# A two-layer decoder trunk on one core: attention steps respaced, rotary chain split, one weight tile requested earlier, output written in four pieces

## The chip, the core and the metric

The kernel runs on one core of a Trainium2 chip. A core has a matrix engine (TensorE, PE in the profile, with its weight loads as PEld), a vector engine (VectorE, DVE), an activation engine (ScalarE, ACT), a general engine (GpSimd, POOL) and a queue engine that issues transfers (SyncE, SP). The engines run side by side, each takes its own instructions in order, and they wait for each other by semaphores. The metric is the device time of one execution in microseconds; lower is better.

## What is computed

Two layers run over 256 tokens of width 2048, in float32. Of the reference this is the part that the change touches:

```python
h = rms_norm(x, attn_norm[l])
z = h @ w_in[l]
za, zq, zk, zv, zc = jnp.split(z, SPLIT_IDX, axis=-1)
ya = gmlp_mixer(za, ...)            # gelu, layer norm, 128 x 128 token mixing
yb = diff_attention(zq, zk, zv, lam, cos, sin)   # 4 heads, q and k turned by cos and sin
yc = short_conv_mixer(bg, cg, hc, conv_w[l])
x = x + (mix * mix_norm[l]) @ w_out[l]           # mix = group norms of ya, yb, yc
h = rms_norm(x, ffn_norm[l])
x = x + (jax.nn.silu(h @ w_gate[l]) * (h @ w_up[l])) @ w_down[l]
...
return rms_norm(x, final_norm)
```

`cos` and `sin` are taken of position times inverse frequency. `rms_norm` divides each token by the root of the mean of its squares, so each token has one scale `r`.

## The kernel before

**Weights.** All weights (some 420 MB) come from HBM once, as tiles of 512 by 512 numbers (1 MB each, `wf`), at most four of them in SBUF. Each tile is cut into two halves. For each half ACT rounds the weights (`wh`, line 169), DVE takes the difference to the exact ones (`wl`, line 170), and PE makes 12 matmuls of 512 columns (lines 220 to 222): for two token blocks of 128 and two rows of blocks, activations high part times `wh`, times `wl`, and activations low part times `wh`. One half with its 12 matmuls is called a step here, and the steps are numbered from 0. `wh` and `wl` have five buffers, so ACT can start the half of step n + 5 when PE has finished step n.

**Order of the work.** Eight steps make one chunk of 512 output columns of the first projection. Its chunks come in the order v, v (steps 0 to 15, interleaved), q and k of head pair 0 (16 to 31), q and k of head pair 1 (32 to 47), the gMLP's second half (48 to 55), the convolution's three parts (56 to 79) and the gMLP's first half (80 to 87). Then come the output projection and the feed-forward part. All the smaller work stands in one list (`pending`, filled by `later(fn, key, wait, gap)`): after each step `step()` takes at most one entry off its front, no sooner than `wait` steps after it was put there and `gap` steps after the last one ran; `need(key)` runs the list until an entry is done.

**What the scheduler does.** The kernel text is not the order of the program. A scheduler that knows the dependencies places the instructions on the engines, and it may pull an instruction ahead of another one on the same engine that stands earlier in the text.

**Attention of a head pair** (`attention`, line 633 on). Four entries `scores` (line 647: product `sp` of keys `bok` and queries `boq`; then mask, maximum, exponent and normalisation, `se` and `st`, on DVE and ACT), then five entries `turn`: transposes `ap` on PE, a copy, products `op` with the values (line 679), group norms with two small POOL instructions (lines 339 and 340). `bok` and `boq` are made by ACT and DVE copies of 32 partitions (lines 456 and 458). The gMLP's `vg` (gelu, line 727), its statistics (`bst`, `mv`), POOL's power `rs` and the normalised `vn` (line 737, then POOL's lines 740 and 741) fall beside the scores of pair 1.

**Start.** `load_weights` and the loads of the transposed input quarters (`xt`, line 308) are issued by SP in the order of the text. POOL works out the rotary angles in some fifty small instructions (`rotary_tables`, lines 346 to 385), and then the token scales `r` (`token_scales`, by `rstd`, lines 339 and 340), for which `v` on ACT (line 707) and `rq` on DVE (line 608) wait.

**End.** After the last products, for each of the two token blocks: residual add and squares (lines 884 and 886), sum, POOL's scale and power, a scaling of two halves of 1024 columns by DVE and ACT (lines 895 and 897), and two transfers of 512 KB (line 898).

Of the kernel before, what the change touches and what calls it, by code (L numbers as in the profile page):

```python
# [11 lines left out]
F32 = mybir.dt.float32  # L12
# [3 lines left out]
ALU = mybir.AluOpType  # L16
AX = mybir.AxisListType

P = 128
D = 2048  # L20
S = 256
NT = S // P
L = 2
CW = 512
# [3 lines left out]
RMS_EPS = 1e-6  # L28
# [25 lines left out]
def trunk_kernel(ctx: ExitStack, tc, x, positions, w_in, gmlp_ln_g, gmlp_ln_b,  # L54
# [8 lines left out]
    nc = tc.nc  # L63
# [75 lines left out]
    def load_weights(n):  # L139
        while state["load"] < min(n, len(wsrc)):  # L140
            i = state["load"]
            wf = wfp.tile([P, 4, CW], F32, tag="wf", name=f"wf{i}")
            w = 2 if i < 4 else 4
            for k in range(0, 4, w):
                nc.sync.dma_start(out=wf[:, k:k + w], in_=wsrc[i][:, k:k + w])
            wfull[i] = wf
            state["load"] += 1
# [41 lines left out]
    def later(fn, key=None, wait=0, gap=0):  # L189

        pending.append((fn, key, clock["now"] + wait, gap))
# [112 lines left out]
    for c in range(NX):  # L304
        xt = blk([P, 4, S], f"xt{c}")
        th, tl = blk([P, 4, S], f"tha0_{c}", F32R), blk([P, 4, S], f"tla0_{c}", F32R)
        for k in range(0, 4, 2):
            nc.sync.dma_start(out=xt[:, k:k + 2], in_=x_t[c, :, k:k + 2])
            if c == 0:
                if k == 0:  # L310
                    nc.sync.dma_start(out=gT, in_=gains)
                load_weight_part(0, 1 + k, 2 + k)
                if k == 0:
                    load_weight_part(0, 2, 3)
            g = [gT[:, 4 * c + kk:4 * c + kk + 1] for kk in range(4)]
            for kk in range(k, k + 2):
                if c == 0:
                    nc.vector.tensor_scalar(th[:, kk], xt[:, kk], g[kk], None, op0=ALU.mult)
                else:
                    nc.scalar.activation(th[:, kk], xt[:, kk], AF.Copy, scale=g[kk])  # L320
            if c == 0:
                split_weights(1 + k // 2)
            for kk in range(k, k + 2):
                nc.vector.scalar_tensor_tensor(tl[:, kk], xt[:, kk], g[kk], th[:, kk].bitcast(F32),
                                               op0=ALU.mult, op1=ALU.subtract)
            if c == 1 and k == 0:
                tabs = load_tables()
        stat[("a0", c)] = (th, tl)
        done.add(("a0", c))
        load_weights(min(c + 1, 3))  # L330

    mask = cpool.tile([P, 2 * P], F32, name="mask")
    nc.gpsimd.memset(mask, 0.0)
# [3 lines left out]
    def rstd(dst, src, scale, eps, n):  # L337

        nc.gpsimd.tensor_scalar(dst, src, scale, eps, op0=ALU.mult, op1=ALU.add)
        nc.gpsimd.tensor_tensor(dst, dst, neghalf[:, :n], op=ALU.pow)  # L340

    def rotary_tables(pos_i, frq):
        V = nc.gpsimd

        def axpy(dst, a, c, b):
            V.tensor_scalar(prod, a, c, None, op0=ALU.mult)
            V.tensor_tensor(dst, prod, b, op=ALU.add)

        pos = spool.tile([P, NT], F32, name="pos", bufs=1)
        V.tensor_copy(pos, pos_i)  # L350
        tmp = blk([P, 8, NT * 64], "rtmp")
        ang, far, n, acc, rem, prod = (tmp[:, j, :] for j in range(6))
        for t in range(NT):
            V.tensor_scalar(ang[:, t * 64:(t + 1) * 64], frq, pos[:, t:t + 1], None, op0=ALU.mult)
        big = 2.0 ** 18
        V.tensor_scalar(far, ang, 1.0 / big, MAGIC, op0=ALU.mult, op1=ALU.add)
        V.tensor_scalar(far, far, MAGIC, None, op0=ALU.subtract)
        axpy(ang, far, -big, ang)
        cs = _parts(TWO_PI, 8, 3)
        cs.append(float(np.float32(TWO_PI - sum(cs))))  # L360
        fm = _far_mod()
        fs = _parts(abs(fm), 8, 3)
        fs.append(float(np.float32(abs(fm) - sum(fs))))
        if fm < 0:
            fs = [-v for v in fs]

        def turns(src, scale):
            V.tensor_scalar(n, src, scale / TWO_PI, MAGIC, op0=ALU.mult, op1=ALU.add)
            V.tensor_scalar(n, n, MAGIC, None, op0=ALU.subtract)

        turns(far, fm)
        V.tensor_scalar(rem, far, fs[0], None, op0=ALU.mult)
        axpy(rem, n, -cs[0], rem)
        for j in range(1, 4):
            axpy(rem, far, fs[j], rem)
            axpy(rem, n, -cs[j], rem)
        turns(ang, 1.0)
        for j in range(4):
            axpy(ang, n, -cs[j], ang)
        V.tensor_tensor(ang, ang, rem, op=ALU.add)  # L380
        turns(ang, 1.0)
        for j in range(4):
            axpy(ang, n, -cs[j], ang)
        lim = 3.1415925
        V.tensor_scalar(ang, ang, lim, -lim, op0=ALU.min, op1=ALU.max)

        def waves():
            with tc.issue_after(state["dve"].ins):
                nc.vector.scalar_tensor_tensor(acc, ang, -1.0, ang, op0=ALU.mult, op1=ALU.max)
                nc.vector.tensor_scalar(acc, acc, -1.0, math.pi / 2, op0=ALU.mult, op1=ALU.add)  # L390
            with tc.issue_after(state["act"].ins):
                nc.scalar.activation(sinT.rearrange("p t d -> p (t d)"), ang, AF.Sin)
                nc.scalar.activation(cosT.rearrange("p t d -> p (t d)"), acc, AF.Sin)

        return waves


    neglam = cpool.tile([P, L], F32, name="neglam")
# [19 lines left out]
    def layer_loads(l):  # L418
        lc = [blk([P, 2, CW], f"lc{l}_{j}") for j in range(3)]
        wT = lc[0][:, 0].rearrange("p (g c) -> p g c", g=4)  # L420
        lng, lnb = lc[1][:, 0], lc[1][:, 1]
        cw = [lc[0][:, 1], lc[2][:, 0], lc[2][:, 1]]

        def gmlp():
            nc.sync.dma_start(out=wT, in_=ws_t[:, l])
            nc.sync.dma_start(out=lng, in_=gmlp_ln_g[l].rearrange("g c -> (g c)").partition_broadcast(P))
            nc.sync.dma_start(out=lnb, in_=gmlp_ln_b[l].rearrange("g c -> (g c)").partition_broadcast(P))
            nc.gpsimd.affine_select(out=wT, in_=wT, compare_op=ALU.is_ge, fill=0.0, base=0,
                                    pattern=[[0, 4], [1, P]], channel_multiplier=-1)

        later(gmlp, gap=2)
        def conv():
            for k in range(3):
                nc.sync.dma_start(out=cw[k], in_=conv_w[l, k].partition_broadcast(P))

        later(conv, gap=2)
        return lng, lnb, cw, wT
# [148 lines left out]
        later(lambda c=c: load_x(c), wait=5)  # L586
    for c in range(NX):
        later(lambda c=c: sum_squares(c, ssq))
    waves = rotary_tables(*tabs)

    for l in range(L):

# [18 lines left out]
                    nc.vector.tensor_scalar(rt[:, t, j, 1], sinT[:, t], sc, None, op0=ALU.mult)  # L611

        later(token_scales, ("r", l))
        lng, lnb, cw, wT = layer_loads(l)
        if l == 0:
            later(lambda: lambdas(load_lambda()))
        later(rotary_scales, ("rt", l), wait=17 if l == 0 else 0)

        def rotate(acc, j, name):

# [14 lines left out]
        def attention(pair, qT, kT, v):  # L635
# [52 lines left out]
                parts.append((scores, values, mixed))  # L688
            order = [(hh, i) for hh in range(2) for i in range(NT)]
            for hh, i in order:  # L690
                later(lambda i=i, f=parts[hh][0]: f(i), wait=2)
            for n in range(5):
                def turn(n=n):
                    if n:
                        parts[order[n - 1][0]][2](order[n - 1][1])
                    if n < 4:
                        parts[order[n][0]][1](order[n][1])
                later(turn)
            block_transposed(oy, M, key, 64 + 16 * l + 4 * (1 + pair), wait=2)

        vn = mx = xc_ = yconv = None
# [177 lines left out]
    flush()  # L879
    ov = out[0].rearrange("(t p) d -> p t d", p=P)  # L880
    c = NX - 1
    for t in range(NT):
        xc = xs[:, t, c * CW:(c + 1) * CW]
        nc.vector.tensor_tensor(xc, xc, acc[t], op=ALU.add)
        junk = spool.tile([P, CW], F32, tag="junk", name="junk", bufs=1)
        nc.scalar.activation(junk, xc, AF.Square, accum_out=ssq[:, t, c:c + 1])
        r = spool.tile([P, 2], F32, tag="rl", name="rl")
        nc.vector.tensor_reduce(r[:, 0:1], ssq[:, t], axis=AX.X, op=ALU.add)
        rstd(r[:, 1:2], r[:, 0:1], 1.0 / D, RMS_EPS, 1)
        rr = r[:, 1:2]  # L890
        nc.vector.tensor_tensor(xf[t][1][:, 1], xc, fin[1][:, 1], op=ALU.mult)
        for h in range(2):
            o = xf[t][h]
            if h == 0:
                nc.vector.tensor_scalar(o, o, rr, None, op0=ALU.mult)
            else:
                nc.scalar.activation(o, o, AF.Copy, scale=rr)
            nc.sync.dma_start(out=ov[:, t, 2 * h * CW:2 * (h + 1) * CW].rearrange("p (c n) -> p c n", c=2), in_=o)


_INS = ["x", "positions", "w_in", "gmlp_ln_g", "gmlp_ln_b", "lambda_q1", "lambda_k1", "lambda_q2",
# [39 lines left out]
```

## Time and profile before

| | |
|---|---|
| median of 3 runs | 2122.61 us (2120.73 to 2123.92) |
| profiled execution | 2121.89 us, of which its span 2119.8 us |
| PE busy | 2098.0 us, 99% of the span |
| DVE, ACT, POOL busy | 1559.2, 1137.6, 201.0 us |
| read from HBM | 423.19 MB |

The span runs from the first instruction to the last event of the profiled execution; the execution's own time is 2.1 us longer. PE is busy nearly throughout, so what can be gained without taking work off PE lies where PE waits: at the start, at the end and at the few places where its next operand is late. The view of waits lists these, the timeline places them, and the windows give the clock that PE was granted (1.00 is the upper level of 2.4 GHz).

### The profile page before, as it was taken

How to read it: one execution, taken by the hardware profiler on the slowest of the kernel's cores; microseconds unless marked ns; L12 is line 12 of the kernel's file. 1: busy time of each engine (PE TensorE's matmuls, PEld its weight loads, DVE VectorE, ACT ScalarE, POOL GpSimd, SP SyncE). 2: the span in 40 equal slices, each digit the busy share in tenths (PEclk: the TensorE clock that was granted, in tenths of full speed). 3: DMA queues.
4: the chain of work that ended last, by engine and by line, in shares of the span. 5: the costliest groups of instructions: out<-in, count | busy, mean ns of one | idle time of the engine just before them, and what ended most of it. 6: DMA issues, size and time to landing. Idle time of an engine off the chain costs nothing.

```text
span 2119.8 us, 25036 instructions
## 1 busy us (share of the span) xinstructions
PE 2098.0 (99%) x9264; PEld 1735.2 (82%) x9264; DVE 1559.2 (74%) x1926; ACT 1137.6 (54%) x1479; POOL 201.0 (9%) x199
## 2 busy tenths in 40 slices
PE   8999999999999999999999999999999999999998
PEld 7887888888888888888888878888888888888886
DVE  5787778877567775678767878788775678756874
ACT  6556468555444543454755664675554454534453
POOL 6123410000000000000001234000000000000002
PEclk9999999999999999999999999999999999999999
DMA  8654555676556656566565445556655566655663
GB/s 317 240 177 161 179 211 176 219 250 218 199 180 245 220 203 221 205 222 204 204 235 190 160 158 197 201 186 247 219 200 220 207 220 215 227 204 208 212 231 123
DMA packets 83013, 440.54 MB, mean 208 GB/s; under 512 B 13518, under 2 KB 25294, under 8 KB 34252
## 3 DMA queue, kind: packets, MB, share of 16 engines
q1 hardware_dynamic: 79580, 427.16, 55.3%
q0 software_dynamic: 3168, 11.54, 3.2%
q8 instruction: 72, 1.18, 0.2%
q14 instruction: 49, 0.40, 0.1%
q10 hardware_dynamic: 144, 0.26, 0.0%
HBM read 423.19 MB, written 2.10 MB: 201 GB/s over the span
## 4 chain that ended last, share of the span: by engine, by line
PE 86%; POOL 2%; DVE 2%; ACT 1%; issue 1%; DMA 0%; SPq 0%; POOLq 0%; ACTq 0%
PE acc L221 14%; PE acc L220 14%; PE acc L222 14%; PE c L221 13%; PE c L220 13%; PE c L222 13%; PE p L221 2%; PE p L220 2%; PE p L222 2%; DVE wl L170 1%; PE op L679 0%; ACT wh L169 0%; DMA x<-xh 0%; ACT bom L456 0%; POOL gsq L573 0%
## 5 line engine op out<-in xcount | busy, mean ns | idle before, releaser
L170 DVE TENSOR_TENSOR wl<-wf,wh 128x1024 fp32r<-128x1024 f32 (+1 forms) x836 | 1029.5, 1245 | 455.7 <-ACT wh L169 451.6
L169 ACT CAST wh<-wf 128x1024 fp32r<-128x1024 f32 (+1 forms) x836 | 868.4, 1050 | 837.4 <-PE acc L222 397.9
L220 PE MATMUL c<-wh,thf 128*128 128x512 f32 x1144 | 445.0, 389 | 0.0
L221 PE MATMUL c<-wl,thf 128*128 128x512 f32 x1144 | 445.0, 389 | 0.0
L222 PE MATMUL c<-wh,tlf 128*128 128x512 f32 x1144 | 445.0, 389 | 0.0
L220 PE MATMUL acc<-wh,tha 128*128 128x512 f32 x704 | 280.6, 399 | 1.4 <-ACT wh L169 1.4
L221 PE MATMUL acc<-wl,tha 128*128 128x512 f32 x704 | 275.4, 391 | 2.9 <-DVE wl L170 2.9
L222 PE MATMUL acc<-wh,tla 128*128 128x512 f32 x704 | 275.3, 391 | 0.0
L220 PE MATMUL acc<-wh,thd 128*128 128x512 f32 x704 | 273.9, 389 | 0.0
L221 PE MATMUL acc<-wl,thd 128*128 128x512 f32 x704 | 273.9, 389 | 0.0
L222 PE MATMUL acc<-wh,tld 128*128 128x512 f32 x704 | 273.9, 389 | 0.0
L220 PEld LDWEIGHTS c<-wh,thf 128*128 128x128 f32 x1144 | 214.7, 188 | 44.6
L222 PEld LDWEIGHTS c<-wh,tlf 128*128 128x128 f32 x1144 | 214.8, 188 | 44.5
L221 PEld LDWEIGHTS c<-wl,thf 128*128 128x128 f32 x1144 | 214.8, 188 | 44.5
L221 PEld LDWEIGHTS acc<-wl,tha 128*128 128x128 f32 x704 | 133.0, 189 | 31.1 <-DVE wl L170 4.2
L220 PEld LDWEIGHTS acc<-wh,tha 128*128 128x128 f32 x704 | 132.7, 189 | 29.2 <-ACT wh L169 1.9
L222 PEld LDWEIGHTS acc<-wh,tla 128*128 128x128 f32 x704 | 132.7, 188 | 28.4
L220 PEld LDWEIGHTS acc<-wh,thd 128*128 128x128 f32 x704 | 132.2, 188 | 27.4
L222 PEld LDWEIGHTS acc<-wh,tld 128*128 128x128 f32 x704 | 132.2, 188 | 27.4
L221 PEld LDWEIGHTS acc<-wl,thd 128*128 128x128 f32 x704 | 132.2, 188 | 27.4
L175 POOL DMA_DIRECT2D wf<-in_w_up_dram x22 | 19.4, 880 | 1324.3 <-DVE wl L170 1324.3
L221 PE MATMUL acc<-wl,thm 128*128 128x512 f32 x256 | 99.7, 390 | 0.1
(193 smaller groups left out, 1867.9 us busy)
## 6 DMA issues: line engine op xcount, KB each, us to landing
wf<-in_w_gate_dram SPq DMA_DIRECT2D x88, 1024.0 KB, 4.8
wf<-in_w_up_dram SPq DMA_DIRECT2D x88, 1024.0 KB, 6.3
wf<-in_w_down_dram SPq DMA_DIRECT2D x88, 1024.0 KB, 4.9
wf<-in_w_in_dram SPq DMA_DIRECT2D x84, 1024.0 KB, 4.8
wf<-in_w_out_dram SPq DMA_DIRECT2D x32, 1024.0 KB, 4.7
wf<-in_w_up_dram POOLq DMA_DIRECT2D x22, 512.0 KB, 5.7
bod<-btd SPq DMA_DIRECT2D x352, 32.0 KB, 1.9
wf<-in_w_in_dram SPq DMA_DIRECT2D x6, 512.0 KB, 8.1
```

The lines of the kernel that those rows point to most:

```text
L169: state["act"] = nc.scalar.copy(wh[:, k:k + w], wf[:, k:k + w])
L170: state["dve"] = nc.vector.tensor_tensor(wl[:, k:k + w], wf[:, k:k + w], wh[:, k:k + w].bitcast(F32), op=ALU.subtract)
L175: nc.gpsimd.dma_start(out=wf, in_=wsrc[onto[j][1]][:, 0:2], accum_op=ALU.add)
L220: nc.tensor.matmul(acc, xh[k], wh[:, k, :], start=first and k == 0, stop=False)
L221: nc.tensor.matmul(acc, xh[k], wl[:, k, :], start=False, stop=False)
L222: nc.tensor.matmul(acc, xl[k], wh[:, k, :], start=False, stop=last and k == 1)
```

## The change

Four edits, none of which changes what is computed:

- **Attention.** The `scores` entries of head pair 1 get `gap=2` (every other step), and the first `turn` of both pairs gets `gap=2`.
- **Rotary.** `rotary_tables` returns its last part as a function `near`, which is put on the list behind `token_scales`; `rotary_scales` of layer 0 gets `wait=20` in place of 17.
- **Start.** `load_weights(min(c + 2, 4))` in place of `min(c + 1, 3)`: each weight tile is requested one input quarter sooner.
- **End.** The sum over the first three quarters is made ahead of the last products; the last quarter's part is added by one DVE instruction with the constant, and POOL keeps the power alone. Each block's output goes out in four pieces of 512 columns, three scaled by DVE and sent by SP, one scaled and sent by ACT.

```diff
--- before.py
+++ after.py
@@ -327,7 +327,7 @@
                 tabs = load_tables()
         stat[("a0", c)] = (th, tl)
         done.add(("a0", c))
-        load_weights(min(c + 1, 3))
+        load_weights(min(c + 2, 4))
 
     mask = cpool.tile([P, 2 * P], F32, name="mask")
     nc.gpsimd.memset(mask, 0.0)
@@ -374,15 +374,17 @@
         for j in range(1, 4):
             axpy(rem, far, fs[j], rem)
             axpy(rem, n, -cs[j], rem)
-        turns(ang, 1.0)
-        for j in range(4):
-            axpy(ang, n, -cs[j], ang)
-        V.tensor_tensor(ang, ang, rem, op=ALU.add)
-        turns(ang, 1.0)
-        for j in range(4):
-            axpy(ang, n, -cs[j], ang)
-        lim = 3.1415925
-        V.tensor_scalar(ang, ang, lim, -lim, op0=ALU.min, op1=ALU.max)
+
+        def near():
+            turns(ang, 1.0)
+            for j in range(4):
+                axpy(ang, n, -cs[j], ang)
+            V.tensor_tensor(ang, ang, rem, op=ALU.add)
+            turns(ang, 1.0)
+            for j in range(4):
+                axpy(ang, n, -cs[j], ang)
+            lim = 3.1415925
+            V.tensor_scalar(ang, ang, lim, -lim, op0=ALU.min, op1=ALU.max)
 
         def waves():
             with tc.issue_after(state["dve"].ins):
@@ -392,7 +394,7 @@
                 nc.scalar.activation(sinT.rearrange("p t d -> p (t d)"), ang, AF.Sin)
                 nc.scalar.activation(cosT.rearrange("p t d -> p (t d)"), acc, AF.Sin)
 
-        return waves
+        return near, waves
 
 
     neglam = cpool.tile([P, L], F32, name="neglam")
@@ -586,7 +588,7 @@
         later(lambda c=c: load_x(c), wait=5)
     for c in range(NX):
         later(lambda c=c: sum_squares(c, ssq))
-    waves = rotary_tables(*tabs)
+    near, waves = rotary_tables(*tabs)
 
     for l in range(L):
 
@@ -611,10 +613,12 @@
                     nc.vector.tensor_scalar(rt[:, t, j, 1], sinT[:, t], sc, None, op0=ALU.mult)
 
         later(token_scales, ("r", l))
+        if l == 0:
+            later(near)
         lng, lnb, cw, wT = layer_loads(l)
         if l == 0:
             later(lambda: lambdas(load_lambda()))
-        later(rotary_scales, ("rt", l), wait=17 if l == 0 else 0)
+        later(rotary_scales, ("rt", l), wait=20 if l == 0 else 0)
 
         def rotate(acc, j, name):
 
@@ -688,14 +692,14 @@
                 parts.append((scores, values, mixed))
             order = [(hh, i) for hh in range(2) for i in range(NT)]
             for hh, i in order:
-                later(lambda i=i, f=parts[hh][0]: f(i), wait=2)
+                later(lambda i=i, f=parts[hh][0]: f(i), wait=2, gap=2 * pair)
             for n in range(5):
                 def turn(n=n):
                     if n:
                         parts[order[n - 1][0]][2](order[n - 1][1])
                     if n < 4:
                         parts[order[n][0]][1](order[n][1])
-                later(turn)
+                later(turn, gap=0 if n else 2)
             block_transposed(oy, M, key, 64 + 16 * l + 4 * (1 + pair), wait=2)
 
         vn = mx = xc_ = yconv = None
@@ -879,23 +883,28 @@
     flush()
     ov = out[0].rearrange("(t p) d -> p t d", p=P)
     c = NX - 1
+    ends = [spool.tile([P, 4], F32, tag="rl", name="rl") for t in range(NT)]
+    for t in range(NT):
+        r = ends[t]
+        nc.vector.tensor_reduce(r[:, 0:1], ssq[:, t, :c], axis=AX.X, op=ALU.add)
+        nc.vector.tensor_scalar(r[:, 1:2], r[:, 0:1], 1.0 / D, RMS_EPS, op0=ALU.mult, op1=ALU.add)
     for t in range(NT):
         xc = xs[:, t, c * CW:(c + 1) * CW]
         nc.vector.tensor_tensor(xc, xc, acc[t], op=ALU.add)
         junk = spool.tile([P, CW], F32, tag="junk", name="junk", bufs=1)
+        r = ends[t]
         nc.scalar.activation(junk, xc, AF.Square, accum_out=ssq[:, t, c:c + 1])
-        r = spool.tile([P, 2], F32, tag="rl", name="rl")
-        nc.vector.tensor_reduce(r[:, 0:1], ssq[:, t], axis=AX.X, op=ALU.add)
-        rstd(r[:, 1:2], r[:, 0:1], 1.0 / D, RMS_EPS, 1)
-        rr = r[:, 1:2]
+        nc.vector.tensor_scalar(r[:, 2:3], ssq[:, t, c:c + 1], 1.0 / D, r[:, 1:2], op0=ALU.mult, op1=ALU.add)
+        nc.gpsimd.tensor_tensor(r[:, 3:4], r[:, 2:3], neghalf[:, :1], op=ALU.pow)
+        rr = r[:, 3:4]
         nc.vector.tensor_tensor(xf[t][1][:, 1], xc, fin[1][:, 1], op=ALU.mult)
-        for h in range(2):
-            o = xf[t][h]
-            if h == 0:
+        for n in (0, 3, 1, 2):
+            o = xf[t][n // 2][:, n % 2]
+            if n < 3:
                 nc.vector.tensor_scalar(o, o, rr, None, op0=ALU.mult)
             else:
                 nc.scalar.activation(o, o, AF.Copy, scale=rr)
-            nc.sync.dma_start(out=ov[:, t, 2 * h * CW:2 * (h + 1) * CW].rearrange("p (c n) -> p c n", c=2), in_=o)
+            (nc.sync if n < 3 else nc.scalar).dma_start(out=ov[:, t, n * CW:(n + 1) * CW], in_=o)
 
 
 _INS = ["x", "positions", "w_in", "gmlp_ln_g", "gmlp_ln_b", "lambda_q1", "lambda_k1", "lambda_q2",
```

SP's first transfers, in rows of the program: `xt` are the input quarters, `wf` the weights (the first tile in parts of 256 KB, later ones in halves of 512 KB), `pos_i` and `frq` the positions and frequencies. Before:

```order
L308 DMA xt_109<-in_x_t_dram 128x512
L153 DMA wf_80<-in_w_in_dram 128x512
L308 DMA xt_138<-in_x_t_dram 128x512
L298 DMA pos_i<-in_positions_dram 128x2x1
L300 DMA frq<-in_inv_freq_dram 128x64
L308 DMA xt_138<-in_x_t_dram 128x512
L145 DMA wf_155<-in_w_in_dram 128x1024 x2
```

And now:

```order
L308 DMA xt_109<-in_x_t_dram 128x512
L153 DMA wf_80<-in_w_in_dram 128x512
L145 DMA wf_138<-in_w_in_dram 128x1024 x2
L308 DMA xt_141<-in_x_t_dram 128x512
L298 DMA pos_i<-in_positions_dram 128x2x1
L300 DMA frq<-in_inv_freq_dram 128x64
L308 DMA xt_141<-in_x_t_dram 128x512
```

Both halves of the second weight tile moved from behind the second input quarter, the positions and the frequencies to ahead of them.

On POOL, the end of the rotary chain (`rtmp`) and the token scales `r` of layer 0. Before:

```order
L347 TENSOR_TENSOR rtmp<-rtmp 128x128
L346 TENSOR_SCALAR rtmp<-rtmp 128x128
L347 TENSOR_TENSOR rtmp<-rtmp 128x128
L385 TENSOR_SCALAR rtmp<-rtmp 128x128
L339 TENSOR_SCALAR r<-tot 128x2
L340 TENSOR_TENSOR r<-r,neghalf 128x2
L428 AFFINE_SELECT lc_0_242<-lc_0_242 128x512
```

And now:

```order
L347 TENSOR_TENSOR rtmp<-rtmp 128x128
L346 TENSOR_SCALAR rtmp<-rtmp 128x128
L347 TENSOR_TENSOR rtmp<-rtmp 128x128
L387 TENSOR_SCALAR rtmp<-rtmp 128x128
L339 TENSOR_SCALAR r<-tot 128x2
L340 TENSOR_TENSOR r<-r,neghalf 128x2
L430 AFFINE_SELECT lc_0_223<-lc_0_223 128x512
```

Nothing moved here: the instructions of `near` stand ahead of `r` in the program as they did before.

On DVE, where the gMLP's second `vn` meets the scores of head pair 1 in layer 0 (layer 1 has the same rows). Before:

```order
L653 TENSOR_TENSOR se<-sp,mask 128x2x128
L737 TENSOR_SCALAR vn<-vg,mv,rs 128x128 x4
L654 TENSOR_REDUCE st<-se 128x2
L170 TENSOR_TENSOR wl_1647<-wf_1595,wh_1646 128x1024
L653 TENSOR_TENSOR se<-sp,mask 128x512
L658 RECIPROCAL st<-st 128x2
L654 TENSOR_REDUCE st<-se 128x2
L659 TENSOR_TENSOR st<-st,neglam 128x1
L660 TENSOR_SCALAR se<-se,st 128x128
L170 TENSOR_TENSOR wl_1678<-wf_1595,wh_1677 128x1024
```

And now:

```order
L741 TENSOR_SCALAR vn<-vg,mv,rs 128x128 x4
L460 COPY bok<-btk 32x2x4x32 x4
L170 TENSOR_TENSOR wl_1634<-wf_1587,wh_1633 128x1024
L170 TENSOR_TENSOR wl_1652<-wf_1587,wh_1651 128x1024
L657 TENSOR_TENSOR se<-sp,mask 128x2x128
L658 TENSOR_REDUCE st<-se 128x2
L170 TENSOR_TENSOR wl_1681<-wf_1637,wh_1680 128x1024
L662 RECIPROCAL st<-st 128x2
L663 TENSOR_TENSOR st<-st,neglam 128x1
L664 TENSOR_SCALAR se<-se,st 128x128
L665 SCALAR_TENSOR_TENSOR se<-se,st 128x128
```

The scores now have a weight half between them, and DVE's last four key copies `bok`, which stood ahead of the gMLP's statistics, stand behind the second `vn`; on PE the four `sp` pairs stand ahead of steps 60, 62, 64 and 66 where they stood ahead of 58, 59, 60 and 61.

## Rows read from the trace of the kernel before

**Rows 1.** The page's busy time: us, share of the span, instructions.

```profile
PE 2098.0 (99%) x9264; PEld 1735.2 (82%) x9264; DVE 1559.2 (74%) x1926; ACT 1137.6 (54%) x1479; POOL 201.0 (9%) x199
```

**Rows 2.** Waits of PE, the longest: us in total, times, longest.

```profile
PE op L679 <- DVE st L658: 7.9, 2, 4.1
```

**Rows 3.** Windows: length, busy us of PE, PEld, DVE, ACT, POOL, granted clock, DMA share, GB/s.

```profile
189.00:212.00 23.00, 19.23 (x82) 15.38 (x81) 15.40 (x28) 11.69 (x29) 6.45 (x10) 0.93 0.51 183
1240.00:1262.00 22.00, 17.89 (x75) 14.24 (x74) 14.26 (x24) 11.54 (x28) 6.15 (x9) 0.92 0.52 188
```

**Rows 4.** Timeline of PE (start, us, idle before): begins of steps 1, 4; step 14.

```profile
10.32 0.39 PE L220 MATMUL acc<-wh,tha 128*128 128x512 f32 x1
20.92 0.39 PE L220 MATMUL acc<-wh,tha 128*128 128x512 f32 x1
48.12 0.39 PE L220 MATMUL acc<-wh,tha 128*128 128x512 f32 x1
49.87 0.50 PE L221 MATMUL acc<-wl,tha 128*128 128x512 f32 x1 [1.37 <-DVE wl L170]
```

**Rows 5.** Timeline of POOL and DVE: rotary chain and token scales of layer 0.

```profile
9.33 0.91 POOL L350 CAST pos<-pos_i 128x2 f32<-128x2 int32 x1 [7.45 <-DMA pos_i<-in_positions_dram]
30.94 1.38 POOL L346 TENSOR_SCALAR rtmp<-rtmp 128x128 f32<-128x128 f32 x1
45.51 0.53 POOL L346 TENSOR_SCALAR rtmp<-rtmp 128x128 f32<-128x128 f32 x1
48.10 0.21 DVE L608 TENSOR_SCALAR rq<-r 128x1 f32<-128x1 f32 x2 [9.24 <-POOL r L340]
```

**Rows 6.** DMA totals of the windows 0 to 8.2, 7 to 8.2, 8.2 to 10.

```profile
DMA packets 1142, 1.83 MB, mean 223 GB/s; under 512 B 276, under 2 KB 276, under 8 KB 1142
DMA packets 298, 0.48 MB, mean 400 GB/s; under 512 B 64, under 2 KB 64, under 8 KB 298
DMA packets 607, 0.52 MB, mean 291 GB/s; under 512 B 409, under 2 KB 409, under 8 KB 607
```

**Rows 7.** Timeline of PE: begins of steps 39, 45, 61 and 67.

```profile
120.28 0.58 PE L220 MATMUL acc<-wh,tha 128*128 128x512 f32 x1
140.36 0.39 PE L220 MATMUL acc<-wh,tha 128*128 128x512 f32 x1
186.39 0.58 PE L220 MATMUL acc<-wh,tha 128*128 128x512 f32 x1
211.88 0.39 PE L220 MATMUL acc<-wh,tha 128*128 128x512 f32 x1
```

**Rows 8.** Timeline of all engines: begin of step 55, last key copies, gMLP statistics.

```profile
167.43 1.19 DVE L458 COPY bok<-btk 32x256 f32<-32x256 f32 x4
167.56 0.39 PE L220 MATMUL acc<-wh,tha 128*128 128x512 f32 x1
171.75 0.69 ACT L727 ACTIVATE vg<-acc,r 128x512 f32<-128x512 f32 x1
177.20 2.15 POOL L740 TENSOR_TENSOR vn<-vn,lc 128x512 f32<-128x512 f32 x1 [1.29 <-PE sp L647]
179.42 1.28 POOL L741 TENSOR_TENSOR vn<-vn,lc 128x512 f32<-128x512 f32 x1
182.13 1.11 DVE L737 TENSOR_SCALAR vn<-vg,mv,rs 128x128 f32<-128x128 f32 x4 [2.57 <-POOL rs L340]
```

**Rows 9.** Timeline: convolution's last sum on POOL; begin of step 84 on PE.

```profile
247.06 3.27 POOL L776 TENSOR_TENSOR xh<-xh,x 128x1024 f32<-128x1024 f32 x1
259.95 0.39 PE L220 MATMUL acc<-wh,tha 128*128 128x512 f32 x1
```

**Rows 10.** Timeline of the end: four transfers, POOL's last scale, last scaling.

```profile
2109.49 6.22 SPq L898 DMA_DIRECT2D out_dram<-xf  x4
2113.27 0.19 POOL L339 TENSOR_SCALAR rl<-rl 128x1 f32<-128x1 f32 x1 [4.59 <-DVE rl L888]
2114.13 1.15 ACT L897 ACTIVATE xf<-xf,rl 128x1024 f32<-128x1024 f32 x1 [1.14 <-POOL rl L340]
```

## The prediction

> **What bounds the kernel now.** I read the page first: PE is busy for 2098.0 of 2119.8 us [rows 1], so nearly all that can be won lies where PE waits. The waits of PE come next: the longest is that of the products `op` for the scores of head pair 1, 7.9 us in two waits, one per layer [rows 2]. The windows around these show a granted clock of 0.93 and 0.92 [rows 3], so each wait also leaves PE for a while at its lower level of 1.2 GHz. The timeline of the start shows two more losses: steps 1, 2 and 3 take 20.92 - 10.32 = 10.60 us where three steps of 12 matmuls at 2.72 us take 8.16, a loss of 2.44; and step 14 waits for `wl` until 49.87 [rows 4]. That `wl` stands behind `rq` on DVE, and `rq` waited 9.24 us for the token scales, which POOL makes after the rotary chain that began when the positions landed, at 9.33 [rows 5].
>
> **The start and the rotary chain.** The second weight tile is now requested ahead of the second input quarter, and 1.05 MB land sooner, when PE needs them. I take the whole 2.44 us as gone for steps 1 to 3; the later quarters have slack of a step or more. But it does not reach the end, because step 14 is bound to a time and not to PE: it waits for `r`. The edit that was to bring `r` forward changes nothing in the program: on POOL the instructions of `near` still stand ahead of `r`. What does change is when the chain begins. The queue works in order: in the first 8.2 us 1.83 MB moved, about what is queued ahead of the positions (the first tile, the first quarter, the gains, half of the second quarter: 1.9 MB), and the small packets of positions and frequencies came just behind [rows 6]. Now 1.05 MB more stand ahead of them; at 400 GB/s [rows 6] that is 2.6 us, so the chain begins near 12.0. Not all of it arrives at the other end. POOL's instructions take 1.38 us beside a busy DVE and 0.53 for the same one when DVE sits waiting [rows 5]; DVE runs dry when it did before, so the part of the chain pushed past that point runs at the shorter duration. Of 2.6 us I let 1.6 remain (bounds 0.5 and 2.6). `wl` of step 14 then comes at 49.87 + 1.6 = 51.5, while PE stands ready at 48.12 - 2.44 + 0.39 = 46.1: a wait of 5.4 us in place of 1.37. That is longer than the two waits that took the clock down, so I charge what those cost beyond the wait, 1.7 us (below; bounds 0 and 2.0). The start as a whole is +1.6 + 1.7 = **+3.3 us** (+0.5 to +4.6).
>
> **Scores of pair 1, what goes.** From the begin of step 39 to that of step 45 head pair 0 takes 140.36 - 120.28 = 20.08 us, for the same PE work for which pair 1 takes 211.88 - 186.39 = 25.49 [rows 7]. The difference of 5.41 is the wait (3.8) and 1.6 of low clock: 0.07 of 23 us below full clock is 1.6 too [rows 3]. In layer 1 the wait is 4.1 [rows 2] and the clock 0.08 of 22 us [rows 3], 1.8: 5.9. Together **-11.3 us**. With a weight half between two scores' DVE work, `st` is ready several steps before its product, so nothing of this should be left.
>
> **Scores of pair 1, what comes.** DVE's last four key copies now stand behind the gMLP's second `vn`, and every `sp` waits for them; PE's first `sp` stands ahead of step 60. PE gets there, unstalled, five steps after the begin of step 55: 167.56 + 13.6 = 181.2 on the clock of the trace before [rows 8]. The copies: ACT can cast for step 59 once step 54 is done, near 167.8; cast 1.05, table load 1.28, so `vg` begins near 170.1 instead of 171.75. From there to the end of the second `vn` the chain through statistics, POOL's power, POOL's two multiplies and the second power took 182.13 + 1.11 - 171.75 = 11.5 us [rows 8], and the four copies take 1.19 [rows 8]: 182.8. PE waits 182.8 - 181.2 = 1.6 us in each layer, **+3.3 us** in all. It is short of the waits that lowered the clock. Low bound 0.8 a layer, if POOL's first multiply takes the 1.28 of the second and not 2.15 [rows 8]; high bound 3.4, if the second takes 2.15 and another 0.9 is lost at the powers. Behind the waiting `sp` all of PE is queued.
>
> The same instruction takes POOL longer beside a busy DVE (1.38 against 0.53, and 2.15 against 1.28) [rows 5, 8]. The Trainium skill, SBUF — State Buffer, section "SBUF: two separate sides", says why this may be: the two share a pair of ports, held for a whole instruction, and the other blocks. By that rule both multiplies would be held up here, since DVE now has copies and a weight half beside them; in the trace one of the two is.
>
> **Convolution and first gMLP half.** On DVE two convolution products, two adds, both norm sums and both norm products now stand in one row between the weight halves of steps 83 and 84, where a weight half lay between the norms. They wait for POOL's last convolution sum. That ended at 247.06 + 3.27 = 250.3, and PE began step 84 at 259.95 [rows 9], 9.6 us later. The attention's tail pushes the convolution's first product some 0.6 us back against PE, and two mixing products of 0.7 move in between, so about 10 us remain. Eight instructions of DVE stand in the row; at about 1.1 us each, as the four-part `vn` of 1.11 [rows 8], an estimate, they take 9 us. It should just fit; for lateness that is passed on I take **+0.7 us** (0 to +4).
>
> **The end.** POOL's scale of 0.19 us with its hand-over, 0.27, leaves the chain; the last scaling, 1.15 us for 1024 columns on ACT [rows 10], is cut into pieces, so the first piece starts its transfer some 0.5 us sooner; the last of four issues ended at 2109.49 + 6.22 = 2115.7 and the span 4.1 us later [rows 10]. DVE's three pieces end about when ACT's one did. I take **-0.7 us** (-1.2 to 0). ACT's own transfer has nothing behind it. The other moved loads wait for nothing that PE uses at once and cost nothing; their cover is the queue's slack of several steps.
>
> **The sum.** +3.3 - 11.3 + 3.3 + 0.7 - 0.7 = -4.7 us. Low ends: +0.5 - 11.3 + 1.6 + 0 - 1.2 = -10.4; high ends: +4.6 - 11.3 + 6.8 + 4 + 0 = +4.1. The profiled execution took 2121.89 us, 0.72 below the median of the runs; against that median the forecast is 2122.61 - 4.7 = 2117.9 us.
>
> **Rivals.** (a) The split works after all: `r` comes before `near`. Then the start gives back 2.44 and step 14's wait of 1.37 [rows 4]: -3.8 in place of +3.3, and 2110.8 us. For it speaks the text; against it the order on POOL. (b) The key copies are in time and `sp` does not wait: 3.3 less, 2114.6. It needs the chain of rows 8 to be 1.6 us shorter than it was. (c) The waits come back: 3.4 us in place of 1.6 at each first `sp`, twice 1.8, and 2 us more in the convolution's row, +5.6, 2123.5: no change. (d) POOL is held up more than before: DVE now has copies and a weight half beside both of POOL's multiplies, not beside one, so that the second goes from 1.28 to 2.15 in each layer [rows 8], twice 0.9 more: 2119.7. For it speaks that one of the two had the longer time already; against it that the other did not, with DVE busy at 74% over all [rows 1]. (This is the case that the section named above, of the Trainium skill's SBUF — State Buffer, describes.) (e) Slower: the convolution's row starves PE. [...] With 3 us of wait in both layers it costs 9.4 more: 2127.3. For it speaks that the row has no weight half in it; against it the 9.6 us of lead that the trace has.
>
> **How the numbers follow.** 0.2% of the median is 4.2 us, about what a measurement of this kernel can tell from no change; so faster means below 2118.4. Chances: forecast 0.42, its own range 2115 to 2121, half of it on either side of 2118.4; (a) 0.06; (b) 0.13, faster; (c) 0.16, no change; (d) 0.15, mostly no change; (e) 0.08, slower. Faster: 0.06 + 0.13 + 0.23 + 0.03 = 0.45; same 0.47; slower 0.08. The range from 2112.5 to 2123.5 leaves out (a), (e) and some of (b) and (c).
>
> **What would show it.** Right: no wait of `op` for `st`; one wait of some 5 us at step 14 for `wl`, behind POOL's `r` near 49.7, and a lower granted clock after it; steps 1 to 3 without waits; a wait of 1 to 2 us at the first `sp` of pair 1 in each layer, released by DVE. Wrong: `r` near 40 us; no wait at `sp`, or one over 3.5; a wait at step 84 for `wl`. The forecast falls if the long wait does not lower the clock, or if the positions land as early as before.

## The result, and the profile after

| | before | after |
|---|---|---|
| median, us | 2122.51 (4 runs, 2120.73 to 2123.92) | 2133.61 (4 runs, 2132.61 to 2134.70) |
| ratio, with its 95% interval | | 1.0053 (1.0035 to 1.0070) |
| span of the profiled execution, us | 2119.8 | 2131.8 |

The change made the kernel slower by about 11 us. The forecast was 2117.9 with a range up to 2123.5: wrong in its sign and outside its range.

First the page's line of busy times and the longest waits of PE after the change (us in total, times, longest), which answer to [rows 1, 2]:

```profile
PE 2102.5 (99%) x9264; PEld 1739.0 (82%) x9264; DVE 1574.4 (74%) x1934; ACT 1136.1 (53%) x1479; POOL 186.1 (9%) x197
PE sp L651 <- DVE bok L460: 10.6, 2, 5.3
PE acc L221 <- DVE wl L170: 8.8, 4, 3.8
```

The wait of `op` for `st` is gone from the list, as intended. In its place stands a wait of the products `sp` for DVE's key copies `bok`, 5.3 us in each layer, and the waits for `wl` have grown from 2.9 to 8.8 us. The windows around the first `sp` of pair 1 answer to [rows 3] (length, busy us of PE, PEld, DVE, ACT, POOL, granted clock, DMA share, GB/s):

```profile
180.00:205.00 25.00, 19.68 (x85) 16.17 (x84) 20.31 (x40) 11.75 (x20) 5.91 (x5) 0.93 0.36 129
1232.00:1262.00 30.00, 24.68 (x104) 20.16 (x104) 23.66 (x46) 15.35 (x28) 7.04 (x6) 0.89 0.39 139
```

PE is idle there for 5.32 us in each layer, where it was idle for 3.77 and 4.11 us in the windows at the old place, and the granted clock is down again.

Where the 12.0 us of span come from is read by comparing when PE begins the same piece of work in the two traces:

| up to | before | after | lag | added by the stretch |
|---|---|---|---|---|
| step 16 (start) | 55.22 | 57.90 | +2.68 | +2.68 |
| step 73 (scores of pair 1, layer 0) | 228.20 | 232.43 | +4.23 | +1.55 |
| step 84 (convolution, layer 0) | 259.95 | 266.54 | +6.59 | +2.36 |
| step 96 | 293.06 | 299.18 | +6.12 | -0.47 |
| last `op` of pair 1, layer 1 | 1258.55 | 1282.71 | +7.84 | +1.72 |
| first `mxp`, layer 1 | 1281.22 | 1309.25 | +11.71 | +3.87 |
| last step's last product | 2111.06 | 2122.76 | +11.70 | 0 |
| end of the span | 2119.8 | 2131.8 | +12.0 | +0.3 |

(The last `op` and the first `mxp` stand six steps later in the program than before; six steps of 2.72 us are taken off their lag.) So the scores of pair 1, which were to give 8.0 us back in the two layers, cost 3.3, and the convolution cost 6.2 where 0.7 was forecast. These two places are nearly the whole miss: against the forecast 11.3 and 5.5 us of 16.7.

The timeline of DVE, POOL and PE in layer 0, where the gMLP's norm meets the key copies (start, us, instruction, in brackets the idle time before it and its releaser):

```profile
178.20 2.96 DVE L460 COPY bok<-btk 32x256 f32<-32x256 f32 x3
178.30 1.33 POOL L744 TENSOR_TENSOR vn<-vn,lc 128x512 f32<-128x512 f32 x1 [1.29 <-DVE vn L741]
179.71 1.30 POOL L745 TENSOR_TENSOR vn<-vn,lc 128x512 f32<-128x512 f32 x1
182.37 0.29 DVE L460 COPY bok<-btk 32x256 f32<-32x256 f32 x1
...
184.84 1.11 DVE L741 TENSOR_SCALAR vn<-vg,mv,rs 128x128 f32<-128x128 f32 x4 [0.92 <-POOL rs L340]
185.98 3.20 DVE L460 COPY bok<-btk 32x256 f32<-32x256 f32 x4
186.03 1.36 POOL L744 TENSOR_TENSOR vn<-vn,lc 128x512 f32<-128x512 f32 x1 [1.23 <-DVE vn L741]
187.47 1.26 POOL L745 TENSOR_TENSOR vn<-vn,lc 128x512 f32<-128x512 f32 x1
...
189.33 1.19 PE L651 MATMUL sp<-bok,boq 128*128 128x128 f32 x4 [5.32 <-DVE bok L460]
```

One copy by itself took 0.29 us. The three that begin with POOL's pair took 2.96, which is one copy (0.3) and the whole of POOL's two instructions (2.63); the last four took 3.20. These are the copies that PE waits for. In each group two copies took from 1.26 to 1.36 us, about as long as the POOL instruction beside them; the others took 0.28 or 0.29.

The same pattern stands in the convolution (timeline of DVE, POOL and PE, layer 0):

```profile
238.87 2.46 POOL L778 TENSOR_TENSOR xh<-xh,lc 128x1024 f32<-128x1024 f32 x1
239.09 3.32 DVE L170 TENSOR_TENSOR wl<-wf,wh 128x1024 fp32r<-128x1024 f32 x1
241.27 3.41 POOL L778 TENSOR_TENSOR x<-x,lc 128x1024 f32<-128x1024 f32 x1
242.34 7.68 DVE L543 SCALAR_TENSOR_TENSOR tlm<-bom,gT,thm 128x256 fp32r<-128x256 f32 x3
...
247.29 2.45 POOL L780 TENSOR_TENSOR xh<-xh,x 128x1024 f32<-128x1024 f32 x1
249.94 1.21 DVE L170 TENSOR_TENSOR wl<-wf,wh 128x1024 fp32r<-128x1024 f32 x1
251.08 0.47 DVE L543 SCALAR_TENSOR_TENSOR tlm<-bom,gT,thm 128x256 fp32r<-128x256 f32 x1
251.21 0.50 PE L221 MATMUL acc<-wl,tha 128*128 128x512 f32 x1 [2.07 <-DVE wl L170]
```

The attention's tail (`tlm`, 0.47 us by itself) now lies beside the last three of POOL's five large instructions, and three of them take 7.68 us. The `wl` of step 79 comes out behind them, and PE waits 2.07. In layer 1 the wait is as long, and there the clock fell behind it (timeline of PE, first layer 0, then layer 1):

```profile
251.55 0.40 PE L222 MATMUL acc<-wh,tla 128*128 128x512 f32 x1
...
1305.07 0.79 PE L221 MATMUL acc<-wl,tha 128*128 128x512 f32 x1 [2.02 <-DVE wl L170]
1305.66 0.63 PE L222 MATMUL acc<-wh,tla 128*128 128x512 f32 x1
```

So of the 3.87 us that this stretch lost in layer 1, 2.02 are the wait and most of the rest is the lower clock; in layer 0 the wait is nearly all of the 2.36.

The start (timeline of PE; then the begin of POOL's rotary chain and DVE's wait for the token scales):

```profile
45.55 0.39 PE L220 MATMUL acc<-wh,tha 128*128 128x512 f32 x1
49.77 0.79 PE L221 MATMUL acc<-wl,tha 128*128 128x512 f32 x1 [3.83 <-DVE wl L170]
50.36 0.63 PE L222 MATMUL acc<-wh,tla 128*128 128x512 f32 x1
...
55.84 0.39 PE L220 MATMUL acc<-wh,tha 128*128 128x512 f32 x1
57.90 0.39 PE L220 MATMUL acc<-wh,tha 128*128 128x512 f32 x1
```

```profile
11.76 0.24 POOL L350 CAST pos<-pos_i 128x2 f32<-128x2 int32 x1 [9.87 <-DMA pos_i<-in_positions_dram]
...
48.01 0.21 DVE L610 TENSOR_SCALAR rq<-r 128x1 f32<-128x1 f32 x2 [11.20 <-POOL r L340]
```

The chain began 2.43 us later than before, as the forecast had it, and yet `rq`, which stood at 48.10 before [rows 5], came 0.09 us earlier. PE came 2.57 us sooner to step 14 and waited there, and then ran at the lower clock (0.63 us a matmul in place of 0.39) until 55.5.

### The profile page after: what moved, and what is told of

Read it like the earlier page. It is cut to its first block, busy times and chain, and to the rows that moved or that the text cites. A ratio compares the mean times of both kernels' runs of the same rounds, so it can differ in the third digit from the quotient of the medians.

```text
span 2131.8 us, 25038 instructions
## 1 busy us (share of the span) xinstructions
PE 2102.5 (99%) x9264; PEld 1739.0 (82%) x9264; DVE 1574.4 (74%) x1934; ACT 1136.1 (53%) x1479; POOL 186.1 (9%) x197
## 5 line engine op out<-in xcount | busy, mean ns | idle before, releaser
L170 DVE TENSOR_TENSOR wl<-wf,wh 128x1024 fp32r<-128x1024 f32 (+1 forms) x836 | 1016.8, 1230 | 454.3 <-ACT wh L169 449.9
L220 PE MATMUL acc<-wh,thm 128*128 128x512 f32 x256 | 99.6, 389 | 0.0
```

The costliest lines, as they stand in the source:

```text
L170: state["dve"] = nc.vector.tensor_tensor(wl[:, k:k + w], wf[:, k:k + w], wh[:, k:k + w].bitcast(F32), op=ALU.subtract)
L220: nc.tensor.matmul(acc, xh[k], wh[:, k, :], start=first and k == 0, stop=False)
```

## The experiments

Theory: the slowdown is one of order and of POOL. One shifted step put the key copies behind the gMLP's norm and the attention's tail beside the convolution, and there DVE is held up by POOL. Rivals: the spacing of the scores is itself at fault; or the order alone is, without POOL.

**The spacing of the first transpose of pair 0 undone.**

```diff
-                later(turn, gap=0 if n else 2)
+                later(turn, gap=0 if n else 2 * pair)
```

> One value of the change is undone: the first transpose entry of head pair 0 loses its gap of two steps (that of pair 1 keeps it). In the program the last four key copies of DVE then stand ahead of the gMLP's statistics again, and the scores of pair 1 keep every other step. Theory 'order': the wait of 5.3 us at the first scores product of pair 1 exists because this one shifted step put the key copies behind the second vn, so it goes in both layers, with the low clock behind it: 7 us a layer, 2133.6 - 14 = about 2119.6. The wait of 2.0 us at step 79 for wl may stay or go, since attention's tail comes one step earlier. Rival 'spacing': scores every other step are late by themselves (each shares DVE with a weight half); then a wait for st or sp of 3 us or more stays in each layer and the time is above 2126.

Measured: 2116.79 us (7 runs) against 2123.27 for the kernel before beside it, ratio 0.9969 (0.9958 to 0.9980); 2119.6 was expected. The rows that decide are DVE's copies and PE's longest waits:

```profile
170.31 1.19 DVE L460 COPY bok<-btk 32x256 f32<-32x256 f32 x4
PE acc L221 <- DVE wl L170: 6.7, 5, 3.7
PE op L683 <- ACT aT L675: 0.7, 2, 0.4
```

The last copies stand at 170.31 and not at 185.98, take 1.19 us, and no `sp` waits. From step 55 to step 73 PE takes 226.29 - 170.45 = 55.84 us, against 60.64 before and 62.19 after; the same stretch of layer 1 takes 55.82, against 61.18 before and 62.91 after. The waits at the convolution are gone in layer 0 and 1.1 us in layer 1. "Spacing" falls: scores every other step are worth 4.8 us in layer 0 and 5.4 in layer 1. The whole loss of the changed kernel against this one, 16.8 us, hangs on one entry of pair 0 that runs one step later. The forecast priced what followed for the key copies, but did not name this entry as its source.

**The end of the rotary chain really behind the token scales.**

```diff
+        state["pow"] = nc.gpsimd.tensor_tensor(dst, dst, neghalf[:, :n], op=ALU.pow)
...
-            later(near)
+            def behind():
+                with tc.issue_after(state["pow"].ins):
+                    near()
+            later(behind)
```

> The changed kernel with the last part of the rotary chain held behind the token scales on POOL by an order edge (the text alone did not move it). Theory: step 14 waits for r alone, r then comes when tot does, near 37.8 us in place of 47.97, DVE never runs dry, and the whole 6.9 us that steps 14 and 15 lose now (3.8 us of wait and 3.1 us of low clock) goes: 2133.6 - 6.9 = about 2126.7. Rival: steps 14 and 15 wait for something else as well (the input's squares, the weight tiles), and at least 2 us stay; or the late rotary tables hold up the first q and k and a new wait of 1 us or more appears near step 24.

Measured: 2127.49 us, 6.1 below the changed kernel (7.1 in the span). `r` now ends where its sum lets it, and the window in which the changed kernel lost its clock is full:

```profile
39.20 0.73 POOL L340 TENSOR_TENSOR r<-r,neghalf 128x2 f32<-128x2 f32 x1
44.00:59.00 15.00, 15.00 (x68) 12.43 (x67) 8.61 (x7) 9.49 (x11) 13.62 (x17) 1.00 0.81 289
```

Step 16 begins at 50.95 in place of 57.90, and no new wait appears at the first q and k. So `r` was all that step 14 waited for, and the split of the chain, which the scheduler had undone, is worth 6.9 us once an order edge holds it.

**POOL's two instructions of the gMLP's norm left out.**

```diff
-                    vt = vn[:, :, t, :]
-                    nc.gpsimd.tensor_tensor(vt, vt, lng.rearrange("p (g c) -> p g c", g=4), op=ALU.mult)
-                    nc.gpsimd.tensor_tensor(vt, vt, lnb.rearrange("p (g c) -> p g c", g=4), op=ALU.add)
```

> The changed kernel without POOL's product and sum of the gMLP's norm (gain and bias of vn are left out, two POOL instructions of 128x512 per token block and layer). Theory 'held up beside POOL': DVE's key copies took 0.80 to 0.99 us each beside these two and take 0.30 alone, so that three of them and then four take 0.9 and 1.2 us in place of 2.96 and 3.20; the wait at the first scores product falls from 5.3 to about 1.3 us in each layer, and the span falls by 8 to 11 us. Rival 'order alone': the copies are late because they stand behind the second vn and its powers; then they keep 0.8 us each, or the wait stays above 4 us and the span within 3 us.

Measured in one execution: span 2120.5 us, 11.3 less than after. DVE's copies, at the same place in the order:

```profile
178.43 0.88 DVE L460 COPY bok<-btk 32x256 f32<-32x256 f32 x3
180.53 0.29 DVE L460 COPY bok<-btk 32x256 f32<-32x256 f32 x1
184.11 1.19 DVE L460 COPY bok<-btk 32x256 f32<-32x256 f32 x4
185.44 0.68 PE L651 MATMUL sp<-bok,boq 128*128 128x128 f32 x4 [1.19 <-ACT wh L169]
```

2.96 became 0.88 and 3.20 became 1.19. The wait at the first `sp` fell from 5.3 to 1.2 us in each layer. (The view puts it down to ACT's `wh`, but `sp` begins 0.14 us after the last copy's end at 185.30, as it began 0.15 after it in the changed kernel.) So the order makes a wait of 1.2, and POOL makes 4.1 more. "Order alone" falls.

The Trainium skill, SBUF — State Buffer, section "Who interferes with whom", says that where a VectorE and a GpSimd instruction contend for the shared ports, the one that issues first keeps them for its whole instruction while the other blocks, and that "Issue order, not op shape, decides who blocks." For a copy it makes the contention hang on a two-port mode, which no view here names; the durations agree with it: POOL's product began at 178.30, the copy behind it at 178.50 took 1.29 us, and without POOL a copy takes 0.29.

**The earlier weight tile alone, on the kernel before.**

```diff
-        load_weights(min(c + 1, 3))
+        load_weights(min(c + 2, 4))
```

> The kernel before with one part of the change alone: each weight tile requested one input quarter sooner. Theory: steps 1 to 3 gain 2.4 us, r comes at the same time as before (DVE runs dry as much sooner as the positions land later), step 14 waits 3.8 us and the clock falls, so step 16 begins 2.7 us later than before: +2.7 us, 2125.2. Rival: the low clock is not the load's doing, and the 2.4 us are merely waited out at step 14: 2122.5, no change.

Measured: 2124.94 us against 2123.27, ratio 1.0006 (0.9997 to 1.0016): no difference that can be told. The profile shows the mechanism all the same: step 14 begins at 45.70 in place of 48.12, waits 3.97 us, the clock falls, and step 16 begins at 56.76, 1.5 us later than before. The 2.7 expected were too much by the time that the clock stayed low: beyond the wait it cost 56.76 - 45.70 - 5.44 - 3.97 = 1.65 us here, and 57.90 - 45.55 - 5.44 - 3.83 = 3.08 in the changed kernel.

**Both mendings.** The diffs of the first two together.

> The changed kernel with both mendings: the first transpose entry of head pair 0 without its gap, and the end of the rotary chain held behind the token scales. Theory: the two losses are at different places and each is gone as it was alone, 14 + 2.8 and 6.9 us: from e1's 2116.8 another 6.9 off, about 2110. Rival: with the early part of the layer 7 us sooner, transfers or POOL's work meet other steps and at least 3 us come back; 2113 or more.

Measured: 2110.32 us (2110.19 to 2110.51), ratio to the kernel before 0.9942 (0.9929 to 0.9954): 12 to 13 us faster than before, 23 faster than after. The two gains add up.

**POOL's convolution in smaller instructions**, on the changed kernel.

```diff
-                    nc.gpsimd.tensor_tensor(src, src, cw[k].unsqueeze(1).to_broadcast([P, NT, CW]), op=ALU.mult)
+                    for t, n in cuts:
+                        nc.gpsimd.tensor_tensor(src[:, t, n], src[:, t, n], cw[k][:, n], op=ALU.mult)
```

(`cuts` are the four pieces of 128x256; the two sums are cut in the same way.)

> The changed kernel with one size changed: POOL's five convolution instructions of 128x1024 are cut into four of 128x256 each. Theory 'one instruction of the one is held up for a whole one of the other': DVE's tlm of 128x256, which took 2.56 us each beside POOL's 2.5 us instructions (0.47 alone), take 1.0 to 1.3 each beside pieces of about 0.65, attention's tail is done 4 us sooner, and the wait of 2.0 us at step 79 for wl is gone in both layers: the span falls by 4 to 5 us. Rival 'the two share by amount of work': the same POOL work slows DVE as long as it lasts, tlm stay above 2 us each and the wait stays.

Measured in one execution, timeline of DVE and POOL at the same place:

```profile
239.29 2.48 POOL L780 TENSOR_TENSOR x<-x,lc 128x256 f32<-128x256 f32 x2
241.08 2.72 DVE L543 SCALAR_TENSOR_TENSOR tlm<-bom,gT,thm 128x256 fp32r<-128x256 f32 x3
241.73 1.80 POOL L780 TENSOR_TENSOR xh<-xh,lc 128x256 f32<-128x256 f32 x2
```

Three `tlm` took 2.72 us in place of 7.68, and the wait at step 79 is gone in both layers: from step 73 to step 84 PE takes 31.75 us, to the hundredth what it took before the change, and from the last `op` to the first `mxp` of layer 1 22.67 in place of 26.54. A short DVE instruction takes about as long as the POOL instruction beside it: 0.96 beside 0.92 here, 2.6 beside 2.5 in the changed kernel. But the span fell by 1.1 and not by 4 to 5: the pieces took POOL some 22 us in each layer in place of 13 to 14, what follows them came late, and PE waits 1.3 us for `wl` near steps 92 and 94 in each layer, so that steps 84 to 96 take 1.9 us longer than after in each; another 1.3 went to a longer low clock after the first `sp` of layer 0, of which 0.7 came back in layer 1. The mechanism is confirmed; of the gain in time only a quarter came.

**Both mendings, with the pieces and with the output in two pieces a block again.**

```diff
-        for n in (0, 3, 1, 2):
+        for h in range(2):
...
-            (nc.sync if n < 3 else nc.scalar).dma_start(out=ov[:, t, n * CW:(n + 1) * CW], in_=o)
+            nc.sync.dma_start(out=ov[:, t, 2 * h * CW:2 * (h + 1) * CW].rearrange("p (c n) -> p c n", c=2), in_=o)
```

> e5 with POOL's convolution in pieces of 128x256 and the output in two pieces of 1024 columns per token block again (the shorter chain ahead of it stays). Theory: some 2 us of small waits around steps 84 to 94 go, and the end takes 8.0 us from the last residual add in place of 8.6 (four pieces took 8.6 to 8.7, the kernel before 8.3): about 2107.5 if e5 gives 2110. Rival: the pieces cost POOL so much more that its sums are late: e5's time or more.

Measured: 2109.71 us (2109.69 to 2109.78), the fastest of all, ratio 0.9939 (0.9927 to 0.9951); of the 2.5 us expected beyond e5 0.6 came. In layer 1 the pieces took away 1.5 us at step 79 and lost 1.2 between steps 84 and 96; in layer 0 they gave 0.2. From the last residual sum to the span's end it takes 2107.7 - 2099.61 = 8.09 us, against 2131.8 - 2123.19 = 8.61 after and 2119.8 - 2111.49 = 8.31 before. So the shorter chain gives 0.2 us and the four pieces take 0.5. The windows of the last transfers show where part of that comes from (GB/s in 40 slices, packets; before, then after):

```profile
GB/s 0 0 0 0 0 0 0 109 423 369 396 437 410 410 410 396 137 0 0 0 0 0 0 0 0 109 423 369 396 437 410 410 396 396 150 0 0 0 0 0
DMA packets 576, 2.10 MB, mean 175 GB/s; under 512 B 64, under 2 KB 64, under 8 KB 576
GB/s 0 0 0 0 0 0 0 0 0 0 310 380 375 380 316 363 369 357 146 0 0 0 0 0 0 211 380 381 380 334 328 386 351 246 0 0 0 0 0 0
DMA packets 1152, 2.10 MB, mean 150 GB/s; under 512 B 128, under 2 KB 128, under 8 KB 1152
```

The same bytes go out in twice as many packets and at 316 to 386 GB/s in place of 369 to 437; for the last block's 1.05 MB that is some 0.3 us, an estimate from the means of these slices (363 and 405).

**Both mendings, without the earlier weight tile.**

```diff
-        load_weights(min(c + 2, 4))
+        load_weights(min(c + 1, 3))
```

> e5 without the earlier request of the weight tiles. Theory: with r early, the 2.4 us that steps 1 to 3 lose without it are no longer waited out at step 14, so they reach the end: 2.4 us above e5. Rival: the load was never worth anything by itself (another wait takes it back): e5's time within 0.5 us in the profile at step 16.

Measured: 2112.76 us, 2.4 above e5 as expected, though the two spans differ by 2.0, of which 52.60 - 51.02 = 1.58 stands at step 16. A wait of 1.25 at step 79 of layer 0, which e5 has not, is made up for by step 96, where the two are 1.58 apart again; the rest is mostly 0.4 in the scores of layer 1, where `op` waits 0.74. With `r` early the earlier tile is worth something; with `r` late it was not.

## Why the prediction was wrong, point by point

**The start** (+3.3 forecast, +2.68 measured): right in size and in place, by two errors that met. `r` was to come 1.6 us later and came 0.09 earlier: DVE ran dry two microseconds sooner (at 36.8 and not at 38.9), and POOL's chain, more of which now ran beside an idle DVE, made up the whole delay of the positions. The step that failed here is "DVE runs dry when it did before". The low clock was charged at 1.7 and cost 3.1. That the text's split changes nothing in the program held, and e2 shows what that cost.

**What goes** (-11.3): held in the main. Without the key copies' wait the stretch of layer 0 takes 4.8 us less than before (e1) where 5.4 were reckoned, and that of layer 1 5.4 where 5.9 were; a new wait of `op` for `aT`, 0.7 in the two layers together, is most of the rest.

**What comes** (+3.3 forecast, 6.4 + 7.1 = 13.4 measured against e1): this is the step that failed most. The order was read rightly, and the wait was named, with its releaser; without POOL it is 1.2 us (e3), near the 1.6 that were forecast. But the copies were priced at 1.19 for four, from a row in which POOL stood idle, and the rule on the shared ports, which the prediction took from the Trainium skill, SBUF — State Buffer, was applied to POOL's instructions alone. It was DVE that stood: 2.0 us in each of the two groups of copies. The forecast looked for POOL's slowness in a place where POOL had already started first. The trace of the kernel before had a row for the other case, beside the second pair of POOL's instructions (timeline of DVE and POOL):

```profile
183.33 1.29 POOL L740 TENSOR_TENSOR vn<-vn,lc 128x512 f32<-128x512 f32 x1 [1.23 <-DVE vn L737]
183.49 2.20 DVE L170 TENSOR_TENSOR wl<-wf,wh 128x1024 fp32r<-128x1024 f32 x1
```

POOL's product began first and took its short 1.29 us; DVE's weight half, 1.23 us elsewhere, took 2.20.

The wait of 5.3 then took the clock down (the `sp` behind e3's wait of 1.2 ran at its full-clock time, 0.68 us in place of 1.19); pair 1 ended at +3.3 in all in place of -8.0. Rival (d) had the right ports and the wrong victim.

**The convolution** (+0.7 forecast, +6.2 measured): the place was wrong. The row ahead of step 84 was in time; what starved was step 79, where the attention's tail, moved six steps back by the spacing, came to lie beside POOL's sums. That the entries behind the spaced ones move six steps back as well was not followed through for DVE and POOL together. With the waits of 2.0 us came the lower clock in layer 1. Rival (e) gave +9.4 for a starved PE near there, by another mechanism, at 0.08.

**The end** (-0.7 forecast, +0.3 measured): the shorter chain gave 0.2; the transfer of smaller pieces, reckoned at nothing, takes 0.5 (e7).

**The rest.** A wait of 0.47 at step 95 that went with the change was not foreseen. The sum's own high end, +4.1, which the stated range left out, lies below the measured +11 as well. In the chances half of the forecast's 0.42 is 0.21 and not 0.23, so faster comes to 0.43; nothing hangs on it.

## What to carry to other kernels

When an instruction is moved on VectorE, look at what GpSimd runs at that moment, and price a short copy or two-input instruction at the time of the GpSimd instruction that it meets; take the price from a row where the two lie side by side. When entries of a list are spaced out, everything behind them moves as well, so check the order of each engine there, not at the spaced entries alone; here one entry one step later cost more than the whole change was to bring. Where a scheduler places instructions, a moved line of text is not a moved instruction until the order shows it.

## What the runs showed of the hardware that was not expected

- DVE held up by POOL: a copy of 0.29 us took up to 1.36, a 128x256 multiply and subtract of 0.47 took up to 2.63, beside POOL instructions of 1.3 and 2.5 us. With POOL's instructions at a quarter of the size it took 0.96.
- A wait of 2.0 us lowered the clock in layer 1 of the changed kernel and not in layer 0 (rows above); without the gMLP norm's two instructions (e3) it was layer 0 that ran at the lower clock behind such a wait, and layer 1 that did not.
- The lower clock after a wait of about 4 us lasted until 55.5 in one program and until 52.8 in another that had waited as long (3.83 and 3.97 us), so the same wait cost 3.1 or 1.65 us beyond itself:

```profile
50.06 0.80 PE L221 MATMUL acc<-wl,tha 128*128 128x512 f32 x1 [3.97 <-DVE wl L170]
52.36 0.63 PE L220 MATMUL acc<-wh,tha 128*128 128x512 f32 x1
52.79 0.46 PE L221 MATMUL acc<-wl,tha 128*128 128x512 f32 x1
53.08 0.40 PE L222 MATMUL acc<-wh,tla 128*128 128x512 f32 x1
```

  (Timeline of PE with the earlier tile alone; the changed kernel's rows stand above, back at 0.39 only at 55.84.) What decides between the two was not tried.
